# A hybrid mixer layer on one core: tokens added by accumulating transfers, DeltaNet's meta products and transposes over the whole array, scores in pieces of 24

## The chip, the cores and the metric

The kernel runs on one core of one Trainium2 chip. The metric is the device time of one execution in microseconds. Engines are named as in the profile: PE (TensorE matmul), PEld (TensorE weight load), DVE (VectorE), ACT (ScalarE), POOL (GpSimd), SP (SyncE, which here only issues transfers).

## The reference, cut to what matters

One layer with a residual add. 512 tokens of width 2048 are put behind 16 learned meta tokens, normalised, and projected to 7,585 columns that feed three mixers side by side: gated DeltaNet (6 heads), GLA (5 heads) and forgetting attention (5 heads). Their outputs, each times a SiLU gate, are concatenated to width 2048 and go through one output projection; its result is added to the tokens, and a final RMSNorm follows.

```python
h = rms_norm(x, norm_w)
proj = (h @ w_in).astype(f32)
...
o_dn  = gated_head_norm(gated_delta_rule_chunked(q_dn, k_dn, v_dn, log_a, beta), dz, dn_norm_w)
o_gla = gated_head_norm(gla_chunked(...), gz, gla_norm_w)
o_fox = forgetting_attention(...) * silu(fz)
o = concatenate([o_dn, o_gla, o_fox], -1)[:, PAD:]
return x + o @ w_out
```

The meta tokens are the first 16 of 528 columns in every mixer. For DeltaNet they give the state with which the first real block starts: `ym = (I + A)^-1 v`, then `state = k^T ym`, on 16 tokens. GLA's `attn` inside a block of 128 weighs each key dimension by a decay of its own; the kernel splits it by distance into levels of 64, 32, 16, 8, 4, 2, 1 and 0.

## The kernel before, in words

**Numbers.** All is float32. The large products run as three products of parts (high x high, low x high, high x low) in a type that TensorE streams at full rate. ScalarE makes the high part (`hp`, `ho`, `wh`: a cast), VectorE the low part (`lp`, `lo`, `wl`: a subtraction). Small products run in plain float32; the profile shows each of those as two matmul records.

**Order of the work.** (1) The tokens are loaded, scaled and split, and the first gate products run (`pz`, `pg`, `pbdz`, `pbgz`). (2) 18 pairs of 128-column projections run by Strassen's scheme with 7 instead of 8 products (`px`), about 94 to 477 us. For DeltaNet's q, k and v a convolution follows, and `token_rows` (line 725) turns each head's 128 x 528 result into rows of tokens: four transposes of 128 columns and, for k and v, one of the 16 meta columns, all into one bank of PSUM, with ScalarE copies between. (3) DeltaNet's triangular inverses are built by levels (`levels`, line 1110, `level64`, line 1154) and its four blocks are run (`state0`, line 1178, makes the state from the meta tokens; `core` and `tail` follow). (4) GLA and attention run, head by head; `gla_levels` (line 1377) emits the score products. In (3) and (4) sixteen single projections (`pbgq`, `pbfq`, `pbgz`, `pbfz`) fill TensorE between dependent steps. (5) The output projection has four column groups of 512. `OUT[0]` to `OUT[3]` take the first heads (`po`; three head pairs for groups 0 to 2, two for group 3), then one more head pair and Strassen products for the rest (`ps`) alternate, and a last product into the same banks as the running sum (`pz`) ends it. Each column group has four 128-token accumulators `acc[tb, cc]` in SBUF.

**Who sets the order.** A planner (`Weave`, line 237) writes out the program at build time. Each piece of work is a chain, a generator that yields operations, lists of operations, events or requests for buffers. The planner prices each operation (`cost`, line 206), tracks when its operands are ready, and picks the chain with the earliest start, where a chain's priority is added, and for TensorE a slack (0.25 us; 3.0 us for `token_rows`, line 854). What it emits is each engine's order on the chip; an engine that the plan misjudged waits there. Line 189 calls a TensorE operation light when it has fewer than 64 output columns or its weights have fewer than 128 rows or columns. Lines 343 to 356 gather light operations in runs: after 1.5 us of heavy work it takes a light operation whose planned ready time has come, and leaves light work when the run with the next list in it would be over 1.5 us long. A change to light costs 0.1 and back 0.2 us in the plan (line 268). A list that a chain yields is emitted as one piece.

**The places of the change.**

- `token_rows`: the meta transpose reads `c[:, 0:NM]`, 16 weight columns, and so is light.
- `dn_group` (line 1088) asks for tiles of `m_s` (16 slots of 128 x 384) and has SP load the meta tokens' values and keys into the first 16 rows of two of them.
- `state0`: three products of 16 x 16 by 16 x 128 (`pym<-vpm,um`), a ScalarE copy, three products with 16 rows (`pym<-ym,kdm`), a copy. All six are light.
- `gla_levels`: the score products are yielded in pieces of CH = 32 (line 92 sets it), two levels to a group; a group of the two small levels has 64 products for two heads, 32 for the last single head.
- `residual` (line 1882): for each accumulator SP loads the 128 x 512 tokens into `acc[tb, cc]`, and `e_res[cc]` tells that the four are there. `add_out` (line 1927) then adds the bank of `po` with VectorE and gives the bank back.
- `out_sums` (line 1801) has GpSimd issue accumulating transfers, 32 in all, that add weight matrices in HBM during stage (2).

Of the kernel before, what the change touches and what calls it, by code (L numbers as in the profile page):

```python
# [88 lines left out]
NXP, SQP, NSL = -0.6, 0.0, 1.5  # L89
LP, LSL = 0.1, 1.0  # L90
EXTRA = ()
NOP, CH, CD = 0, 32, 32
WP, AOP, HDP = 1.0, -0.6, 0.0
EARLY_KP = (3, 4)
STK, KOS, OS0, OSN, OSP = (3, 4, 6, 7), 3, 1, 2, 0.1
# [267 lines left out]
def tile_hybrid_trunk(ctx, tc, xT, xtok, mtok, w_gate, w_first, w_in, w_out, consts, lmask, fin_w, out):  # L363
# [361 lines left out]
    def token_rows(key, c, u):  # L725
        what, h = key
        g, j = divmod(h, H)
        blocks = [slice(b * P, (b + 1) * P) for b in range(NB)]
        dst, dstm, scale, acc_, ev = {"dk": (kds, kms, dl, nks, e_gate), "dv": (vps, vms, br, None, e_keys[g]),
                                      "dq": (None, None, None, nqs, e_gate)}[what]  # L730
        yield ev
        pk = yield Get(bank_s, f"pk{what}{h}", keep=2)
        yield [PE.transpose(pk[:, s], c[:, NM + s.start : NM + s.stop], ident) for s in blocks]
        if acc_ is not None:
            for b, s in enumerate(blocks):
                yield A.activation(u[:, s], pk[:, s], AF.Square, accum_out=acc_[:, b, h : h + 1])
        if dst is not None:
            for b, s in enumerate(blocks):
                yield A.activation(u[:, s], pk[:, s], AF.Copy, scale=scale[:, b, h : h + 1])
            yield SP.dma_start(out=dst[g].rearrange("p (b j) d -> p j b d", j=H)[:, j],  # L740
                               in_=u[:, :S].rearrange("p (b d) -> p b d", b=NB))
            yield PE.transpose(pk[:NM, :P], c[:, 0:NM], ident)
            m = c[:NM, P : 2 * P]
            if acc_ is not None:
                yield A.activation(m, pk[:NM, :P], AF.Square, accum_out=acc_[:NM, NB, h : h + 1])
            yield A.activation(m, pk[:NM, :P], AF.Copy, scale=scale[:NM, NB, h : h + 1])
            yield SP.dma_start(out=dstm[g][:, j], in_=m)
        bank_s.give(pk)
        row_s.give(c)
        sp_of(key).set()  # L750
        if what != "dv":
            {"dk": e_nk, "dq": e_nq}[what][h].set()
# [335 lines left out]
    def dn_group(g):  # L1088
        s = gs[g]
        if g:  # L1090
            yield e_first
        s.xc = yield Get(m_s, f"xc{g}", (P, NN, 32))
        yield e_inv
        yield SP.dma_start(out=s.xc, in_=sc2[N4 * g : N4 * g + N4].rearrange("(n r) (a c) -> (r a) n c", r=4, a=32))
        s.xm, s.um = one((32, H, 32), f"xm{g}"), one((32, H, 32), f"um{g}")
        yield SP.dma_start(out=s.xm, in_=sc2[M0 + H * g : M0 + H * g + H].rearrange("h (a c) -> a h c", a=32))
        s.kdm = yield Get(m_s, f"kdm{g}")
        s.vpm = yield Get(m_s, f"vpm{g}")
        for o, i in ((s.vpm[:NM], vms[g]), (s.kdm[:NM], kms[g])):
            yield SP.dma_start(out=o, in_=i)  # L1100
        yield e_anl[g]
        W.go(levels(g), -0.2, f"levels{g}", LSL)
        if not g:
            e_first.set()
# [5 lines left out]
    def levels(g):  # L1110
        s = gs[g]
        an, xc, xm, um = s.an, s.xc, s.xm, s.um
        uc = yield Get(m_s, f"uc{g}", (P, NN, 32))
        yield V.transpose(uc.rearrange("p n c -> p (n c)"), xc.rearrange("p n c -> p (n c)"))
        pm = yield Get(bank_s, f"pm{g}")
        p3 = pm[:, : NN * 32].rearrange("p (n c) -> p n c", c=32)
        lh = [(slice(64 * q, 64 * q + 32), slice(64 * q + 32, 64 * q + 64)) for q in range(2)]
        mm = [PE.matmul(p3[lo_, n, :], an[hi_, n, lo_], uc[hi_, n, :], start=True, stop=True)
              for n in range(NN) for lo_, hi_ in lh]
        for i in range(0, len(mm), CD):  # L1120
            yield mm[i : i + CD]
        m1 = yield Get(m_s, f"m1{g}", (P, NN, 32))
        for q in range(2):
            yield A.copy(m1[64 * q : 64 * q + 32], p3[64 * q : 64 * q + 32])
        W.go(state0(g), 0.0, f"state{g}")
        yield V.transpose(um.rearrange("p h c -> p (h c)"), xm.rearrange("p h c -> p (h c)"))
        e_um[g].set()
        mm = [PE.matmul(p3[a, n, :], l[lo_, n, :], r[lo_, n, :], start=True, stop=True)
              for n in range(NN) for lo_, hi_ in lh for a, l, r in ((lo_, xc, m1), (hi_, m1, xc))]
        for i in range(0, len(mm), CD):  # L1130
            yield mm[i : i + CD]
        l1 = yield Get(m_s, f"l1{g}", (P, NN, 32))
        yield A.copy(l1, p3)
        bank_s.give(pm)
        m_s.give(m1)
        s.uf = uf = yield Get(big_s, f"uf{g}", (P, NN, P))
        yield G.memset(uf, 0.0)
        for r in range(4):
            c = slice(32 * r, 32 * r + 32)
            yield A.copy(uf[c, :, c], uc[c])  # L1140
        m_s.give(uc)
        for q in range(2):
            yield V.tensor_copy(uf[64 * q : 64 * q + 32, :, 64 * q + 32 : 64 * q + 64], l1[64 * q : 64 * q + 32])
        eh = evs(0, 1)
        for q in range(2):
            W.go(level64(g, q, l1, eh[q]), -0.2, f"l64{g}{q}")
        yield (eh[0], eh[1])
        m_s.give(l1)
        m_s.give(xc)
        e_u[g].set()  # L1150
# [27 lines left out]
    def state0(g):  # L1178
        s = gs[g]
        yield (e_um[g], e_rows[g])  # L1180
        py = yield Get(bank_s, f"pym{g}")
        yield [PE.matmul(py[:NM, hc(j)], s.um[:NM, j, :NM], s.vpm[:NM, j, :], start=True, stop=True) for j in range(H)]
        ym = yield Get(m_s, f"ym{g}")
        yield A.copy(ym[:NM], h3(py)[:NM])
        m_s.give(s.vpm)
        yield [PE.matmul(py[:, hc(j)], s.kdm[:NM, j, :], ym[:NM, j, :], start=True, stop=True) for j in range(H)]
        st = yield Get(m_s, f"s0{g}")
        yield A.copy(st, h3(py))
        bank_s.give(py)
        m_s.give(ym)  # L1190
        m_s.give(s.kdm)
        s.so, s.f = one((P, NB, H), f"so{g}"), one((P, NB, H), f"f{g}")
        W.go(core(g, st), -0.3, f"core{g}")
# [538 lines left out]
    def phase_d():  # L1732
        yield e_c
        W.go(residual(), 0.0, "residual")
        for h in range(DN_HEADS):
            W.go(finish(h, gs[h // H].kd.rearrange("p (b j) d -> p j b d", j=H)[:, h % H], None), -0.05, f"split{h}")
        yield tuple(e_head[h] for h in range(DN_HEADS))
        e_split.set()
        for g in range(2):
            for q in range(3):  # L1740
                r_s.lend(gs[g].kd[:, 4 * q : 4 * q + 4, :].rearrange("p n d -> p (n d)"))
        for kp in ST:
            W.go(seven_heads(kp), HDP, f"heads{kp}")
        W.go(seven_loads(), -0.3, "sloads")
        W.go(seven_operands(), -0.45, "sops")
        yield tuple(e_z[i] for kp in ST for i in (2 * kp, 2 * kp + 1)) \
            + tuple(e_head[i] for kp in LATE for i in (2 * kp, 2 * kp + 1)) + (e_fin,)
        sweep()
        e_d.set()
# [50 lines left out]

    def out_sums():
        for i, (cp, kp) in enumerate((cp, kp) for cp in range(2) for kp in ST):
            p, q = pairs[OS0 + OSN * i : OS0 + OSN * i + 2]
            yield p.done[1]
            t = osum[cp, ST.index(kp)]
            (a, b), (c, d) = (tuple(w_out[2 * cp + n, kp][:, k * S : (k + 1) * S] for k in range(2)) for n in range(2))
            for n, w in ((5, c), (7, d), (6, d), (4, b)):
                yield SP.dma_start(out=t[:, SUMS.index(n)], in_=w)
            for n, w, ev in ((5, a, p.done[6]), (7, c, p.done[7]), (6, t[:, SUMS.index(5)], q.done[1]),
                             (4, t[:, SUMS.index(6)], q.done[6])):  # L1810
                yield ev
                yield G.dma_start(out=t[:, SUMS.index(n)], in_=w, accum_op=ALU.add)
# [69 lines left out]
    def residual():  # L1882
        for cc in range(4):
            for tb in range(4):
                yield OUT[cc][min(1 + tb // 2, len(OUT[cc]) - 1)].op
                acc[tb, cc] = yield Get(op_s, f"acc{cc}{tb}", (P, S), F32)
                yield SP.dma_start(out=acc[tb, cc], in_=xtok[tb * P : (tb + 1) * P, cc * 512 : (cc + 1) * 512])
            e_res[cc].set()

    e_res = evs(*range(4))  # L1890
# [8 lines left out]
    def mm_out(items):  # L1899
# [16 lines left out]
                    yield mm3(ps[tb], wj, oparts[2 * it.kp + j, tb], it is items[0] and j == 0, it is items[-1] and j == 1)  # L1916
            used(w)
        for tb in range(4):
            W.go(add_out(tb, cc, ps[tb]), AOP if cc != 2 else -0.6, f"add{tb}{cc}")
        if items is OUT[3]:  # L1920
            for h in range(DN_HEADS - 2):
                for t in dparts[h]:
                    op_s.give(t)
            yield tuple(e_res.values())
            op_s.move(d_s)

    def add_out(tb, cc, ps):
        yield from add(tb, cc, ps)
# [187 lines left out]
```

## Time and profile before

| | us |
|---|---|
| median of 3 runs | 963.39 (963.23 to 964.7) |
| the profiled execution | 963.21 |
| its span, first to last instruction | 961.4 |
| PE busy in the span | 948.3 |
| DVE busy | 738.5 |
| ACT busy | 581.2 |
| POOL busy | 66.1 |

Busy time of PE counts every stretch in which a matmul is in flight. Matmuls overlap, so the distance between the starts of two matmuls tells more than their durations: a short gap in the queue hides behind the end of the matmul before it. In the order of time each row is the start, the length, the engine, the instruction with what it writes and reads, and in brackets an idle time before it with what ended it. A shape such as 128*16 stands for the rows and columns of the weights. All rows carry line 285, the planner's emitter, so groups are told apart by their tiles.

### The profile page before, as it was taken

What the parts mean: (1) busy time and instruction counts of PE and PEld (TensorE: products, weight loads), DVE (VectorE), ACT (ScalarE), POOL (GpSimd) and SP (SyncE); (2) the same over time, 40 slices, a digit from 0 to 9 for tenths busy, and PEclk for the clock granted to TensorE, in tenths of its full rate; (3) what the DMA queues carried; (4) which work ended last, traced back from release to release, by engine and by line L of the source; (5) the groups of instructions that cost most, each with busy time, mean ns of one, the idle gap of its engine ahead of it and who ended that gap; (6) DMA issues with size and microseconds to landing.
All of it is one profiled execution on the core that took longest, in us unless ns stands there. A gap on an engine that the chain in (4) does not pass through costs nothing.

```text
span 961.4 us, 19098 instructions
## 1 busy us (share of the span) xinstructions
PE 948.3 (99%) x7283; PEld 844.6 (88%) x7283; DVE 738.5 (77%) x1308; ACT 581.2 (60%) x1243; POOL 66.1 (7%) x118
## 2 busy tenths in 40 slices
PE   9999999999999999999999999999999999999996
PEld 7888999999999999999987898878778878888885
DVE  7976888888888887888883665785765886887774
ACT  7855466757756575754432775848737756355445
POOL 0000101001101010110001110101010100000000
PEclk9999999999999999999999999999999999999998
DMA  9933647557786668783178545334323364565414
GB/s 348 367 121 132 162 136 219 163 183 197 198 239 151 208 150 224 183 241 93 67 255 297 167 95 172 135 101 146 117 95 111 130 213 154 195 230 174 151 59 176
DMA packets 92145, 167.20 MB, mean 174 GB/s; under 512 B 16253, under 2 KB 36477, under 8 KB 92052
## 3 DMA queue, kind: packets, MB, share of 16 engines
q1 hardware_dynamic: 87156, 157.31, 49.8%
q0 software_dynamic: 4608, 8.39, 6.3%
q8 instruction: 57, 0.93, 0.4%
q14 instruction: 36, 0.29, 0.1%
q10 hardware_dynamic: 288, 0.27, 0.1%
HBM read 142.33 MB, written 40.39 MB: 190 GB/s over the span
## 4 chain that ended last, share of the span: by engine, by line
PE 94%; DMA 2%; ACT 2%; DVE 1%; issue 0%; DVEq 0%; POOL 0%; SPq 0%; ACTq 0%; POOLq 0%
PE px L285 38%; PE po L285 10%; PE ps L285 8%; PE pbfz L285 6%; PE pz L285 6%; PE pbfq L285 5%; PE pbgz L285 5%; PE pbdz L285 2%; PE pks L285 2%; PE pfa L285 1%; PE pg L285 1%; PE pfw L285 1%; PE pss L285 1%; PE pbgq L285 1%; PE pgo L285 1%; DMA sc<-ab 1%
## 5 line engine op out<-in xcount | busy, mean ns | idle before, releaser
L285 DVE SCALAR_TENSOR_TENSOR lp<-a,hp 128x1024 fp32r<-128x1024 f32 x90 | 110.5, 1228 | 37.6 <-ACT hp L285 35.2
L285 ACT CAST hp<-a 128x1024 fp32r<-128x1024 f32 x90 | 94.5, 1049 | 72.4 <-PE px L285 45.4
L285 PE MATMUL px<-xh,hp 128*128 128x264 f32 x432 | 123.6, 286 | 0.0
L285 PE MATMUL px<-xh,lp 128*128 128x264 f32 x432 | 122.9, 285 | 0.0
L285 PE MATMUL px<-xl,hp 128*128 128x264 f32 x432 | 122.9, 285 | 0.0
L285 PE MATMUL px<-tah,hp 128*128 128x264 f32 x288 | 84.0, 292 | 0.0
L285 PE MATMUL px<-tbh,hp 128*128 128x264 f32 x288 | 82.5, 287 | 0.0
L285 PE MATMUL px<-tbh,lp 128*128 128x264 f32 x288 | 82.1, 285 | 0.0
L285 PE MATMUL px<-tah,lp 128*128 128x264 f32 x288 | 82.0, 285 | 0.0
L285 PE MATMUL px<-tbl,hp 128*128 128x264 f32 x288 | 81.9, 284 | 0.0
L285 PE MATMUL px<-tal,hp 128*128 128x264 f32 x288 | 81.8, 284 | 0.0
L285 PEld LDWEIGHTS px<-xh,hp 128*128 128x128 f32 x432 | 81.4, 188 | 0.0
L285 PEld LDWEIGHTS px<-xh,lp 128*128 128x128 f32 x432 | 81.3, 188 | 0.0
L285 PEld LDWEIGHTS px<-xl,hp 128*128 128x128 f32 x432 | 81.2, 188 | 0.0
L285 ACT CAST hp<-s 128x1024 fp32r<-128x1024 f32 x36 | 37.8, 1049 | 29.7 <-PE px L285 19.8
L285 PEld LDWEIGHTS px<-tbh,hp 128*128 128x128 f32 x288 | 54.3, 189 | 0.1
L285 PEld LDWEIGHTS px<-tbl,hp 128*128 128x128 f32 x288 | 54.3, 189 | 0.0
L285 PEld LDWEIGHTS px<-tah,hp 128*128 128x128 f32 x288 | 54.3, 188 | 0.1
L285 PEld LDWEIGHTS px<-tal,hp 128*128 128x128 f32 x288 | 54.3, 189 | 0.0
L285 PEld LDWEIGHTS px<-tah,lp 128*128 128x128 f32 x288 | 54.2, 188 | 0.0
L285 PEld LDWEIGHTS px<-tbh,lp 128*128 128x128 f32 x288 | 54.2, 188 | 0.0
L285 DVE SCALAR_TENSOR_TENSOR lp<-s,hp 128x1024 fp32r<-128x1024 f32 x36 | 44.0, 1222 | 8.4 <-ACT hp L285 8.4
(406 smaller groups left out, 2639.5 us busy)
## 6 DMA issues: line engine op xcount, KB each, us to landing
a<-in_w_in SPq DMA_DIRECT2D x72, 512.0 KB, 6.3
osum<-in_w_out SPq DMA_DIRECT2D x32, 256.0 KB, 6.2
o<-in_w_out SPq DMA_DIRECT2D x16, 512.0 KB, 3.6
kd<-osum SPq DMA_DIRECT2D x26, 256.0 KB, 3.6
kd<-in_w_out SPq DMA_DIRECT2D x21, 256.0 KB, 3.5
rgz<-in_w_in SPq DMA_DIRECT2D x10, 512.0 KB, 3.3
rfq<-in_w_in SPq DMA_DIRECT2D x10, 512.0 KB, 3.2
rfz<-in_w_in SPq DMA_DIRECT2D x10, 512.0 KB, 3.1
```

Of the source, the lines that this page charges most:

```text
L285: self.pin(op.call(*op.a, **op.kw))
```

## The change

The meta transpose takes the first 128 columns instead of 16 and writes 128 rows of the bank, of which 16 are read as before. The meta products of `state0` run on whole 128 x 128 operands: GpSimd zeroes three tiles, SP loads into two of them as before, and VectorE copies the 32 x 32 inverses into the third, `umf`. CH is 24 instead of 32. `residual` no longer loads the tokens; for the first products of each column group `first_out` has ScalarE copy the bank to `acc` and GpSimd issue a transfer that adds the tokens to it in SBUF. Two more constants are named or made fractional with the values as before.

```diff
-NOP, CH, CD = 0, 32, 32
+SPR = -0.45
+NOP, CH, CD = 0, 24, 32
...
-            yield PE.transpose(pk[:NM, :P], c[:, 0:NM], ident)
+            yield PE.transpose(pk[:, :P], c[:, 0:P], ident)
...
         s.vpm = yield Get(m_s, f"vpm{g}")
+        s.umf = yield Get(m_s, f"umf{g}")
+        for t in (s.umf, s.vpm, s.kdm):
+            yield G.memset(t, 0.0)
...
         yield V.transpose(um.rearrange("p h c -> p (h c)"), xm.rearrange("p h c -> p (h c)"))
+        yield V.tensor_copy(s.umf[:32, :, :32], um)
         e_um[g].set()
...
-        yield [PE.matmul(py[:NM, hc(j)], s.um[:NM, j, :NM], s.vpm[:NM, j, :], start=True, stop=True) for j in range(H)]
+        yield [PE.matmul(py[:, hc(j)], s.umf[:, j, :], s.vpm[:, j, :], start=True, stop=True) for j in range(H)]
         ym = yield Get(m_s, f"ym{g}")
-        yield A.copy(ym[:NM], h3(py)[:NM])
+        yield A.copy(ym, h3(py))
         m_s.give(s.vpm)
-        yield [PE.matmul(py[:, hc(j)], s.kdm[:NM, j, :], ym[:NM, j, :], start=True, stop=True) for j in range(H)]
+        m_s.give(s.umf)
+        yield [PE.matmul(py[:, hc(j)], s.kdm[:, j, :], ym[:, j, :], start=True, stop=True) for j in range(H)]
...
                 acc[tb, cc] = yield Get(op_s, f"acc{cc}{tb}", (P, S), F32)
-                yield SP.dma_start(out=acc[tb, cc], in_=xtok[tb * P : (tb + 1) * P, cc * 512 : (cc + 1) * 512])
             e_res[cc].set()
...
-            W.go(add_out(tb, cc, ps[tb]), AOP if cc != 2 else -0.6, f"add{tb}{cc}")
+            W.go((first_out if items in OUT else add_out)(tb, cc, ps[tb]), AOP if cc != 2 else -0.6, f"add{tb}{cc}")
...
+    def first_out(tb, cc, ps):
+        yield e_res[cc]
+        a = acc[tb, cc]
+        yield A.copy(a, ps)
+        bank_s.give(ps)
+        yield G.dma_start(out=a, in_=xtok[tb * P : (tb + 1) * P, cc * 512 : (cc + 1) * 512], accum_op=ALU.add)
+        need[tb, cc] -= 1
```

More of the change, by code (lines that the diff above doesn't have):

```diff
@@ L1744, in phase_d @@
         W.go(seven_loads(), -0.3, "sloads")
-        W.go(seven_operands(), -0.45, "sops")
+        W.go(seven_operands(), SPR, "sops")
         yield tuple(e_z[i] for kp in ST for i in (2 * kp, 2 * kp + 1)) \
@@ L1802, in out_sums @@
         for i, (cp, kp) in enumerate((cp, kp) for cp in range(2) for kp in ST):
-            p, q = pairs[OS0 + OSN * i : OS0 + OSN * i + 2]
+            p, q = pairs[OS0 + int(OSN * i) : OS0 + int(OSN * i) + 2]
             yield p.done[1]
```

## The prediction

> **What bounds the kernel now.** I read the page first, then the table of stages, then the chain of waits, then the order of time at the places the change touches.
>
> ```profile
> span 961.4 us, 19098 instructions
> ...
> PE 948.3 (99%) x7283; PEld 844.6 (88%) x7283; DVE 738.5 (77%) x1308; ACT 581.2 (60%) x1243; POOL 66.1 (7%) x118
> ```
>
> The profiled execution took 963.21 us, 1.8 us more than its span and 0.18 us less than the median of the three runs, 963.39 us. The sum below is made against 963.21 us. TensorE has work in flight in all but 13 us, most of that at the two ends. So the time can only change with what TensorE's own queue costs: matmul spacing, changes of array shape, and waits inside that queue.
>
> ```profile
> 590.00:771.00 181.00, 178.61 (x1723) 143.52 (x1722) 128.57 (x351) 121.32 (x325) 14.81 (x31) 1.00 0.39 129
> 808.00:852.00 44.00, 44.00 (x193) 35.65 (x192) 36.38 (x60) 18.59 (x28) 0.00 (x0) 1.00 0.51 167
> ```
>
> The columns of the table of stages are the stretch, its length, then the busy time of PE, PEld, DVE, ACT and POOL, the granted clock, the DMA share and GB/s. The GLA and attention stage (590 to 771) leaves TensorE idle for 2.39 us. The output stage (808 to 852), where the accumulating transfers will go, leaves it idle for nothing. GpSimd does nothing there.
>
> **The change part by part.**
>
> *Meta transposes (12, one per DeltaNet key and value head).* Two places in order of time (start, us, engine, work), the first without a wait, the second with one:
>
> ```profile
> 351.35 0.28 PE L285 MATMUL px<-xh,lp 128*128 128x264 f32 x1
> 351.47 0.27 PE L285 MATMUL pkdv<-ident,cv 128*16 128x128 f32 x1
> 351.50 0.36 PE L285 MATMUL px<-xh,hp 128*128 128x264 f32 x1
> 351.70 0.28 PE L285 MATMUL px<-xl,hp 128*128 128x264 f32 x1
> ```
>
> ```profile
> 316.88 0.28 PE L285 MATMUL px<-tah,lp 128*128 128x264 f32 x1
> 317.32 0.28 PE L285 MATMUL pkdv<-ident,cv 128*16 128x128 f32 x1 [0.15 <-ACT u L285]
> 317.35 0.37 PE L285 MATMUL px<-tah,hp 128*128 128x264 f32 x1
> 317.55 0.28 PE L285 MATMUL px<-tal,hp 128*128 128x264 f32 x1
> ```
>
> At 351 it is 0.35 us from the px before the transpose to the second px after it. One px takes 0.12 (351.47 less 351.35), so 0.35 is two px and 0.11 us for the transpose. A 16-column transpose inside a stream of whole-array matmuls therefore costs no more than its own streaming. At 317 the same stretch takes 0.67 us: 0.32 us more, and the bracket names ScalarE's evacuation u. So what these transposes cost is a wait, not their shape.
>
> The Trainium skill says otherwise: "TensorEngine Tiling (Array Packing)", Key Properties, has TensorE drain whenever the tiling mode changes. By that rule each of the 12 would win a pair of switches; the rows at 351 do not show one, and the measurement decides here.
>
> The wait comes from the planner, which writes out TensorE's order. A chain of transposes has a slack of 3.0 us (line 854), so that a chain is picked only when its operands have been ready for a while. But an operation with under 128 weight columns is "light" (line 189). After 1.5 us of heavy work, line 353 picks any light operation whose planned ready time has come, without the slack. And the plan is optimistic here: line 224 prices a 128-element ScalarE copy at 0.21 + 128 x 0.00082 = 0.315 us.
>
> ```profile
> L285 ACT ACTIVATE u<-pkdk,dl 128x128 f32<-128x128 f32 x24 | 7.2, 392 | 0.0
> ...
> L285 ACT ACTIVATE u<-pkdv,br 128x128 f32<-128x128 f32 x24 | 6.9, 368 | 0.6 <-PE pkdv L285 0.6
> ```
>
> ```profile
>   PEld pkdk L285: 0.2, 1
> ```
>
> ```profile
>   PEld pkdv L285: 1.1, 3
> ```
>
> Four such copies precede each meta transpose, so ScalarE ends 4 x 0.053 to 4 x 0.077 = 0.21 to 0.31 us after the plan's time, and TensorE, there on time, waits that long. The last two rows (from the views of the two tiles: who waited for ScalarE's copies, in total and how often) show four such waits of 1.3 us together. With 128 weight columns the transposes are heavy and get the 3.0 us of slack, like the block transposes beside them, which the copies cannot then be late for. Gain: between nothing (the waits land on other work) and 1.3 us; I take 1.2, since the copies are late by 0.3 us and the slack is ten times that. The added weight columns load while the matmul before streams. What the slack costs: a bank and a row buffer are held up to 3 us longer, with nobody in line for them as long as the next pair's convolution comes later than that; I count nothing, and what would be lost if it came sooner is part of the second rival.
>
> *Meta products of DeltaNet (24 matmul records in four groups of six).*
>
> ```profile
> 523.08 0.40 PE L285 MATMUL pbgz<-xh,lbgz 128*128 128x512 f32 x1
> 523.41 0.82 PE L285 MATMUL pym<-vpm,um 16*16 16x128 f32 x6
> 524.16 0.50 PE L285 MATMUL pbgz<-xh,hbgz 128*128 128x512 f32 x1
> 524.50 0.39 PE L285 MATMUL pbgz<-xl,hbgz 128*128 128x512 f32 x1
> ```
>
> ```profile
> 529.22 0.86 PE pym L285 x6
> ...
> 542.27 0.67 PE pks L285 x6
> ...
> 896.96 39.05 PE ps L285 x168
> ```
>
> The second fence is of the chain of waits (start, length, work). It prices whole-array work: 0.67 us for six products of 128 columns, 39.05/168 = 0.232 us for a matmul of 512. The first group stands alone between whole-array matmuls: 523.08 to 524.50 is 1.42 us, where two pbgz and six full products would take 2 x 0.232 + 0.67 = 1.13. Here the change of shape does cost: 0.29 us, in and out together. The others stand next to tiled work that stays, so only their own piece shrinks, from 0.86 to 0.67 in the one shown: 0.19 each at most. The sum lies between 0.29 and 0.29 + 3 x 0.19 = 0.86; I take 0.7 (1.2 if all four gain as the first does). The zeroing and the copy into the padded tile are new:
>
> ```profile
> L285 POOL MEMSET uf<- 128x1536 f32 x2 | 2.8, 1379 | 82.6 <-DMA sc<-ab 82.6
> ```
>
> Each new memset has a quarter of these elements, so between 0.34 and 1.38 us, three ahead of each group's loads, on an engine that had just waited 82.6 us for the inverse. SP's loads of the two meta tiles now wait for GpSimd, and behind them in SP's queue stands group 1's load of the inverse: 1.0 to 4.1 us late. The pbgz pieces around these products are filler that the planner puts into such gaps, so TensorE doesn't see it; without that cover it would cost those microseconds once. The same holds for the tile that now takes one more of 16 slots, and for the copy into it. Counted at nothing.
>
> *Scores in pieces of 24.* The planner prices a 32-wide product at 0.028 us and a run of light work at 1.5 us. Pieces of 32 (0.90 + 0.1 for the switch) do not fit twice, so 64 products run as 32 and 32. Pieces of 24 do (0.10 + 0.67 + 0.67 = 1.44), then 16 in a second run. The number of runs stays two a group, and one for the last pair of heads (24 + 8).
>
> ```profile
> 704.11 1.41 PE pbgz L285 x6
> 705.52 0.69 PE pss L285 x48
> 706.21 1.60 PE pbgz L285 x6
> ```
>
> Six pbgz behind a run take 1.60 instead of 1.41; with the entry as seen at 523 (0.33 from the last pbgz to the first small product instead of 0.23) a run costs 0.3 us beyond its products. The number of runs stays, so zero. Bounds: two runs fewer, -0.6; each of the nine groups split once more, +2.7, which the arithmetic of 1.44 under 1.5 excludes for all but accidents.
>
> *Tokens by accumulating transfers.* 16 vector adds leave, 16 ScalarE copies and 16 GpSimd transfers come, 16 SP loads go.
>
> ```profile
> L285 DVE TENSOR_TENSOR acc<-acc,po 128x512 f32<-128x512 f32 x28 | 17.8, 685 | 2.2 <-PE po L285 2.2
> ```
>
> ```profile
> L285 ACT COPY vt<-pvgv 128x512 f32<-128x512 f32 x5 | 2.9, 584 | 0.0
> ```
>
> ```profile
> osum<-in_w_out POOLq DMA_DIRECT2D x16, 256.0 KB, 6.4
> ```
>
> ```profile
> 845.36 2.48 DVE L285 TENSOR_TENSOR acc<-acc,po 128x512 f32<-128x512 f32 x4
> ```
>
> VectorE saves 16 x 0.685 = 11 us, ScalarE gains 16 x 0.584 = 9.3. Both have room (36.38 and 18.59 of 44 us), and TensorE has no gap there. A bank is free after 0.58 instead of 0.685 us. Accumulating transfers of this size land 6.4 us after their issue, here into HBM; into SBUF is not shown. The last four follow the last four adds, from 845.36. Even one strictly after another they land by 848 + 4 x 6.4 = 874 us, and the next add to those columns comes with the ps work that starts at 896.96. Counted at nothing (0.3 either way for the banks).
>
> Sum: 1.2 + 0.7 + 0 + 0 = 1.9 off the profiled execution's 963.21 is 961.3. A tenth, one bank's 0.1 us, for the case that TensorE reaches one of them too early makes it 961.2, which is 2.2 under the median. Own range: from 0 (no wait gone, first group only, banks against it) to 3.4 (1.3 + 1.2 + 0.6 + 0.3), 959.8 to 963.2.
>
> **The rivals.**
>
> *Waits elsewhere go too.* TensorE's order is planned anew from the first transpose on.
>
> ```profile
> L285 PE MATMUL pkd<-vt,kdt 128*128 128x128 f32 x30 | 4.4, 281 | 1.1 <-DVE gst L285 1.0 <-ACT gst L285 0.2
> ```
>
> Of the 2.39 us idle in 590 to 771 this one product has 1.1. A new order can lose about 2: 959.2. For: such waits exist only because plan and chip disagree. Against: nothing in the change aims at them.
>
> *They come back.* The same the other way, 2 us more: 963.2, no change. For: the slack moves every evacuation of the meta tokens, and with it bank and row buffer.
>
> *Every shape change drains.* If each of the 12 transposes saved the 0.29 us seen at the products, the sum would be 12 x 0.29 + 0.7 = 4.2: 959.0. The rows at 351 speak against it. It is the rule of the Trainium skill named above.
>
> *Slower: ScalarE at the ends of output columns.*
>
> ```profile
> L285 ACT CAST ho<-o 128x1024 fp32r<-128x1024 f32 x14 | 14.7, 1050 | 25.9 <-PE po L285 18.2 <-issue 5.9 <-PE pbfz L285 1.7
> ...
> L285 ACT CAST oh<-gz 128x512 fp32r<-128x512 f32 x5 | 2.7, 617 | 2.9 <-DVE gz L285 2.9
> ```
>
> ```profile
> L285 DVE SCALAR_TENSOR_TENSOR lo<-o,ho 128x1024 fp32r<-128x1024 f32 x14 | 17.1, 1224 | 10.0 <-ACT ho L285 8.6 <-DMA fw<-in_fin_w 1.2
> ```
>
> A weight operand lasts TensorE 24 x 0.232 = 5.57 us; the next needs a cast of 1.05 and a subtraction of 1.22. Four copies ahead make it 2.34 + 1.05 + 1.22 = 4.61, still in time. If five head casts (3.1) queue there too it is 7.7, a wait of 2.1 at each of four columns: 961.2 + 8.4 = 969.6. It decides once more than 0.96 us of other casts stand ahead. Against: ScalarE was busy 18.59 of 44 us there.
>
> **How the numbers follow.** A measurement of this kernel tells about 0.2%, 1.9 us: faster means under 961.46. Forecast 0.50, of which 0.30 falls under that line, as its centre stands 0.3 beneath it. Waits elsewhere go too 0.19, every shape drains 0.06 (both faster). They come back 0.18 (same). ScalarE late 0.07 (slower). That makes 0.55, 0.38 and 0.07. The range takes in the fast rivals' centres with 0.4 to spare and the scores' accidents on the slow side, and leaves out the slow rival and the rest of the fast tails: 958.6 to 963.7.
>
> **What would show it.** Right: the rows pkdk and pkdv with 128*128 alone and no PEld wait for u; pym at 128*128 with about 0.67 us a group; some 15 pss runs behind the first ones, each followed by six-matmul pieces of 1.60; po in one piece of 0.232 us a record; accumulating transfers landed well before acc's next add. Wrong: more pss runs than before, new waits for gst, y or pl, a gap in po, or transposes still waiting.

## The result and the profile after

| | before, us | after, us |
|---|---|---|
| median (11 runs each, taken on one chip) | 963.39 (962.49 to 964.99) | 966.87 (964.12 to 970.53) |
| the profiled execution | 963.21 | 965.08 |
| its span | 961.4 | 963.3 |
| its mean granted clock | 0.997 | 0.995 |

The ratio after to before is 1.0036, interval 1.0025 to 1.0048. The change makes the kernel slower; 961.2 was predicted, with 963.7 as the upper end. The page of after begins:

```profile
span 963.3 us, 19082 instructions
...
PE 945.8 (98%) x7283; PEld 844.5 (88%) x7283; DVE 728.8 (76%) x1294; ACT 588.5 (61%) x1259; POOL 85.7 (9%) x140
```

TensorE has 2.5 us less work in flight than before and yet ends later, so it stands still somewhere. The table of stages, with the two stages of the prediction and the stretch of DeltaNet's inverses:

```profile
520.00:548.00 28.00, 23.64 (x434) 19.39 (x433) 11.53 (x34) 16.73 (x35) 4.01 (x7) 0.94 0.55 161
590.00:771.00 181.00, 177.36 (x1697) 141.95 (x1696) 126.54 (x345) 118.98 (x319) 17.71 (x34) 1.00 0.41 134
808.00:852.00 44.00, 43.92 (x195) 35.45 (x194) 30.51 (x53) 29.59 (x58) 9.75 (x11) 1.00 0.76 203
```

The first of these rows for before:

```profile
520.00:548.00 28.00, 27.83 (x471) 21.96 (x470) 14.37 (x36) 19.24 (x38) 1.86 (x4) 1.00 0.62 205
```

From 520 to 548 TensorE had been idle for 0.17 us and is now idle for 4.36, and the granted clock, full before, is 0.94. GLA and attention lose 3.64 instead of 2.39 us; the output stage loses next to nothing (0.08), as predicted. The chain of waits names the place (start, length, what; the counts are those of the records on the chain, not of all). After:

```profile
521.47 3.83 DMA xc<-sc
...
525.39 0.59 DVE uc L286
...
526.02 0.95 PE pm L286 x48
526.97 1.58 PE pbfq L286 x6
528.55 0.95 PE pm L286 x66
529.50 1.53 PE pym L286 x12
531.04 0.52 PE pm L286 x41
531.56 3.17 issue
534.73 0.96 PE pm L286 x49
535.69 2.69 PE pbfq L286 x6
```

Before:

```profile
515.32 4.97 DMA xc<-sc
...
520.94 0.95 PE pm L285 x48
...
523.48 0.75 PE pym L285 x6
...
525.81 0.95 PE pm L285 x66
...
528.34 0.88 PE pm L285 x48
...
534.10 0.95 PE pm L285 x66
535.05 1.58 PE pbfq L285 x6
...
537.46 0.75 PE pym L285 x6
...
544.47 0.86 PE pym L285 x6
```

`pm` are the 32 x 32 products that build the inverses, per group a list of 48 records (`pm<-uc,an`) and one of 96. Before, the four lists lie from 520.9 to 535.1, with full products between every two. After, VectorE can turn the loaded inverses (`uc`) only later, group 0's by 3.9 and group 1's by 2.0 us. Before:

```profile
520.31 0.58 DVE L285 STREAM_TRANSPOSE uc<-xc 128x384 f32<-128x384 f32 x1 [3.74 <-DMA xc<-sc]
523.40 0.58 DVE L285 STREAM_TRANSPOSE uc<-xc 128x384 f32<-128x384 f32 x1 [1.04 <-DMA xc<-sc]
```

After:

```profile
524.22 0.58 DVE L286 STREAM_TRANSPOSE uc<-xc 128x384 f32<-128x384 f32 x1 [3.83 <-DMA xc<-sc]
525.39 0.58 DVE L286 STREAM_TRANSPOSE uc<-xc 128x384 f32<-128x384 f32 x1 [0.59 <-DMA xc<-sc]
```

The groups are now ready 1.2 instead of 3.1 us apart, and the lists stand close from 524.9 to 535.7: the two short ones together, six `pbfq`, and the two long ones with the `pym` between. In the last of them TensorE stops for 3.17 us, and the row says "issue": it waited for nothing that the profile shows. In TensorE's own view of waits it is the longest of all:

```profile
PE pm L286 <- issue: 3.2, 1, 3.2
PE pkd L286 <- DVE gst L286: 1.9, 2, 1.0
```

Behind the stop six `pbfq` take 2.69 instead of 1.58 us. In the order of time they start 0.43 us apart, where the same product otherwise takes 0.23:

```profile
536.21 0.63 PE L286 MATMUL pbfq<-xl,hbfq 128*128 128x512 f32 x1
536.64 0.63 PE L286 MATMUL pbfq<-xh,lbfq 128*128 128x512 f32 x1
```

That is about half the clock, and the granted clock agrees (it stands behind the busy times):

```profile
534.64:538.06 3.42, 3.33 (x58) 2.64 (x57) 1.32 (x4) 2.28 (x5) 0.35 (x1) 0.50 0.04 12
```

The stop with what follows it costs 3.17 + (2.69 - 1.58) + 0.3 (52 `pm` records start within 0.72 us behind it, 44 within 0.40 ahead of it) = 4.6 us. Without it the profiled execution would have taken 965.08 - 4.6 = 960.5, 0.7 under the prediction. The 1.87 us between the profiled executions are then 4.6 here and 1.25 in GLA and attention, less 4.0: 0.7 at the start and 0.8 behind the last matmul, where nothing was changed, and 2.5 in between.

**The theories.** TensorE's instructions come by a queue of their own:

```profile
q8 instruction: 57, 0.93, 0.4%
```

57 packets of 0.93 MB, 16 KB each, for 14,566 matmuls and weight loads: one packet for about 256 instructions. Counted from 0 over TensorE's rows in order, these and the waits for semaphores among them, the stop lies behind number 8128 = 256 x 30 + 448, and the trace has packet 30 on its way from 532.55 to 533.51. In ordinary stretches the transfer of packet n starts when TensorE is at about 256 n + 150 to 220. Theory 1: the packet was late, because 96 records of `pm` go by in under 1 us. Theory 2: the products themselves stop (operands, banks, load). Theory 3: the loss lies in the new order of the work behind 560 us. (Numbered as in the expectations of the later runs. In those of the first six, theory 2 is late data by the zeroing and the loads behind it, and theory 3 the copies and accumulating transfers at the end.)

### The profile page after: what moved, and what is told of

Read it like the earlier page. It is cut to its first block, busy times and chain, and to the rows that moved or that the text cites. A ratio compares the mean times of both kernels' runs of the same rounds, so it can differ in the third digit from the quotient of the medians.

```text
span 963.3 us, 19082 instructions
## 1 busy us (share of the span) xinstructions
PE 945.8 (98%) x7283; PEld 844.5 (88%) x7283; DVE 728.8 (76%) x1294; ACT 588.5 (61%) x1259; POOL 85.7 (9%) x140
## 4 chain that ended last, share of the span: by engine, by line
PE 92%; DVE 3%; ACT 2%; DMA 1%; issue 1%; SPq 0%; DVEq 0%; POOL 0%; ACTq 0%; POOLq 0%
PE px L286 38%; PE po L286 9%; PE ps L286 8%; PE pbfq L286 6%; PE pz L286 6%; PE pbgz L286 5%; PE pbfz L286 4%; PE pbdz L286 2%; PE pbgq L286 2%; PE pks L286 2%; PE pfa L286 1%; PE pg L286 1%; PE pfw L286 1%; PE pgo L286 1%; PE pss L286 1%; DMA sc<-ab 1%
```

## The experiments

Times are medians; the ratio is to the kernel before on the same chip.

**Each part alone, and all but the first.** Four kernels with one part of the diff each, and one without the transposes.

```diff
-            yield PE.transpose(pk[:NM, :P], c[:, 0:NM], ident)
+            yield PE.transpose(pk[:, :P], c[:, 0:P], ident)
```

> The kernel before with only the whole-array meta transposes. Theory 1, the supply of instructions: with these transposes no longer light, the planner puts the two groups' small pm products close together, and TensorE uses up the instructions that it has at hand; it stands still for 3 to 4 us inside a list of pm products with nothing that it waits for, and its clock is halved for a few us after it. Less the 1.2 us of the waits for u: 965.5 to 967 us. Theory 2, late data at DeltaNet's start (zeroing on GpSimd, loads behind it): nothing of that is here, 962.2 us. Theory 3, ScalarE copies and accumulating transfers at the end: 962.2 us.

> The kernel before with only the padded meta products of state0 and their zeroing. Theory 1: the pm lists stay as far apart as before, no stall, 962.7 us (0.7 less). Theory 2: the stall of 3 to 4 us in pm comes with the zeroing and the later loads, 966 us. Theory 3: 962.7 us.

> The kernel before with only the score pieces of 24. Theories 1 and 2: as many runs of pss as before, 963.4 us, within 1 us. A rival for the 1.5 us that the GLA stage lost: the pieces move the waits for gst and fp, 965 us.

> The kernel before with only the tokens added by accumulating transfers. Theories 1 and 2: TensorE's queue is the same up to the output stage, 963.4 us, within 0.5. Theory 3: 3 us more, 966.4 us, with gaps between po matmuls behind 796 us.

> The changed kernel with the meta transposes left at 16 columns. Theory 1 (supply of instructions): the pm lists are 7 us of other work apart again, no stall; 962 to 963 us. Theory 2 (late data at DeltaNet's start by zeroing and loads): the stall stays, 966 us.

| | us | ratio | interval |
|---|---|---|---|
| transposes alone | 975.5 | 1.0127 | 1.0112 to 1.0142 |
| meta products alone | 962.0 | 0.9989 | 0.9979 to 0.9999 |
| pieces of 24 alone | 976.55 | 1.014 | 1.0127 to 1.0153 |
| tokens alone | 962.64 | 0.9996 | 0.9988 to 1.0005 |
| all but the transposes | 974.28 | 1.0121 | 1.0106 to 1.0136 |

The parts don't add up: two of them cost 12 and 13 us alone, and all four together 3.5. These two and the kernel with all but the transposes lie 8 to 12 us over what was expected. TensorE's waits with the transposes alone:

```profile
PE pm L285 <- issue: 2.3, 1, 2.3
PE ps L285 <- ACT wh L285: 1.7, 1, 1.7
```

With pieces of 24 alone:

```profile
PE pfa L285 <- ACT fp L285: 7.8, 4, 6.4
```

The stop in `pm` goes with the transposes: it is in the changed kernel and in this one, both at number 8128, and in none of the other four (at the border of packet 29 the meta products alone have 0.4 us, all but the transposes 0.3). The transposes alone bring neither zeroing nor copies nor accumulating transfers, so theories 2 and 3 of the first six expectations can't be what makes it. The other losses are waits for ScalarE and VectorE at places that the change doesn't touch. Pieces of 24 move the last attention head's softmax in among the output products, where VectorE has sums of weights and of outputs ahead of it in its queue; TensorE waits 6.4 us up to 810.3. The kernel with all but the transposes has the same wait (6.7 us), the changed kernel doesn't. Part of the losses is the clock: it is half for 13.7 us with the transposes alone and for 10.2 with pieces of 24, against 3.4 in the changed kernel and none in the one before (all ahead of 950 us). So a new order cost up to 13 us, whatever the edit was for, and the same transposes that cost 12 alone gained 7 on top of the other three parts.

**The lists kept apart.** The changed kernel, with group 1's first list held back in the plan until group 0's second has been evacuated.

```diff
+        if g:
+            yield e_l1
         pm = yield Get(bank_s, f"pm{g}")
...
+        if not g:
+            e_l1.set()
```

> The changed kernel, but group 1's first pm list waits in the plan for group 0's second one. No computation is left out, no data comes sooner. Theory 1: no stall, and the clock stays up: the changed kernel's time less 3.4 us of stall and 1 to 1.5 of slow clock, 960 to 962 us. Theory 2: group 1's data are as late as before and TensorE waits for them as long, 965 to 967 us.

Measured: 961.58 (960.74 to 963.44), 0.9985 (0.9977 to 0.9994), the lowest median of all (the meta products alone, 0.9989, are level with it), 5.3 under the changed one (4.9 by the ratios). Its chain has no stop in `pm`:

```profile
528.72 0.95 PE pm L285 x66
...
531.23 0.88 PE pm L285 x48
532.10 2.31 PE pbfq L285 x9
...
535.95 0.68 PE pm L285 x50
```

This speaks for theory 1, but it can't exclude 3, since the order behind is planned anew too.

**Twice the products, in one list or in pieces.** In the kernel before, group 1's second list is issued twice, as one list of 192 records or in pieces of 64. (In the kernel with one list, group 0's second list goes out whole as well.)

```diff
+        again = [PE.matmul(p3[a, n, :], l[lo_, n, :], r[lo_, n, :], start=True, stop=True)
+              for n in range(NN) for lo_, hi_ in lh for a, l, r in ((lo_, xc, m1), (hi_, m1, xc))]
+        mm = again + mm if g == 1 else mm
```

> The kernel before; group 1's 48 second-level pm products are issued twice into the same places (the same values), and all 96 stand in one list. Theory 1: 384 weight loads and matmuls of 7 to 9 ns each in a row are more than TensorE has at hand; it stands still for 2 to 4 us in the midst of the list, at a multiple of 256 instructions, 967 to 969 us. A supply that is not the limit: only the added 96 records at 9 ns, 964.3 us.

> The kernel before with the same 48 added products, but in pieces of 32, between which the planner puts other matmuls. Theory 1: as many instructions, but spread over 5 us and more, so no stall or one under 0.5 us: 0.9 us for the products and 0.3 to 0.6 for the changes of shape, 964.6 to 965 us. If the added work and not its density counted: the same time as the kernel with the 96 in one list.

Measured: 975.5 (1.0139, 1.0122 to 1.0157) and 971.55 (1.0085, 1.0072 to 1.0099). TensorE's longest wait with the one list:

```profile
PE pm L285 <- issue: 2.8, 1, 2.8
```

The stop comes in the one list, at number 8384 = 256 x 31 + 448, and not in pieces, as expected. Both times are 6 us and more over what was expected. Most of both losses is again in waits elsewhere, so the times say little; a test that leaves the order alone was needed.

**The numbers shifted, the order kept.** In these kernels every engine's order is the same as in the kernel they are made from; only TensorE's warm-up at the start is altered: four of its nine full products give way to small ones, unknown to the plan. Each small one is 4 instructions, so the borders of the packets move against the work.

```diff
-        yield [PE.matmul(pw[:, :P], ones, ones, start=True, stop=True) for _ in range(9)]
+        mm = [PE.matmul(pw[:, :P], ones, ones, start=True, stop=True) for _ in range(5)]
+        for o in mm:
+            o.dur *= 9 / 5
+        yield mm
+        q = slice(0, 32)
+        for _ in range(24):
+            W.pin(nc.tensor.matmul(pw[q, q], ones[q, q], ones[q, q], start=True, stop=True))
```

> The changed kernel with the same order of all work; only the warm-up ahead of the first product differs: 5 full products in place of 9, then 24 products of 32*32, so that every later instruction of TensorE has a number higher by 80 (weight loads and matmuls counted alike). The place where a packet of 256 instructions must have come then lies 80 instructions earlier in the work: 4.8 us of work instead of 3.2 lie between the call for packet 30 and its use. Theory 1 (the standstill inside pm is a late packet of instructions): the standstill goes or falls under 1 us, and with it the halved clock behind it; about 962.5 us (961 to 964), 0.995 to 1.000 of the changed kernel's 966.9 or less, hence level with the kernel before. Theory 2 (the standstill belongs to the products themselves, their operands, banks or load): it stays at the same product, 3 us long, and the time stays at 966.9. Theory 3 (the order behind 560 us costs it): 966.9 as well, with the waits of the GLA stage as they were.

> The same with 44 small products, so that the numbers rise by 160. Packet 30 is then needed before the dense part, but packet 31 in it: 3.1 us of work lie between its call and its use. Theory 1: the standstill is back, 2.5 to 3.5 us long, at instruction 256*31+448 = 8384 of TensorE's rows, which is another product than in the changed kernel (224-160 = 96 instructions later in the work); time 965 to 968. Theory 2: it stays at the same product as in the changed kernel. Theory 3: 966.9 in all cases, and no tie to the numbers.

> The kernel before with the whole-array transposes of the meta tokens alone (975.5 us), with the warm-up changed as above so that the numbers rise by 80; the order of all other work stays. 5.5 us of work then lie between the call for packet 30 and its use instead of 3.9. Theory 1: the 2.5 us standstill in pm goes with its slow clock, 3 to 4 us, to about 972; the rest of its loss, the waits for ScalarE and VectorE at 645 to 750 and at 861 to 864, stays, since the order stays. Theory 2: 975.5 with the standstill in place.

Measured: 965.19 (1.0023, 1.0013 to 1.0032), 972.86 (1.0095, 1.0083 to 1.0107) and 972.72 (1.0101, 1.0085 to 1.0117). With 80 the stop is gone, but not by the shift alone: the clock is half from 529.98 to 533.39, between the short and the long lists, and stretches the work in question from the expected 4.8 to 6.2 us. With 160 it is back at number 8384, as expected, at another product than in the changed kernel:

```profile
PE pm L286 <- issue: 2.3, 1, 2.3
```

The two times missed. The altered warm-up costs too much, as the start with 80 shows, and with 160 the clock is also half for 10.2 us from 530.95 on:

```profile
3.56 2.77 PE L537 MATMUL warm<-ones 32*32 32x32 f32 x48
6.26 2.08 PE L286 MATMUL pz<-xh,fhi 128*128 128x512 f32 x4
8.13 1.91 PE L286 MATMUL pz<-xl,fhi 128*128 128x512 f32 x4
```

The first real product starts at 6.26 instead of 5.16 us, and eight of them need 0.45 us each where the full clock gives 0.23. The transposes alone came out near what was expected: 2.8 us less (2.5 by the ratios) with the stop gone, and the waits at 861 us unchanged; here too the clock was half, from 529.58 to 532.99, ahead of the long lists.

**Five and nine products more.** The full warm-up stays, and small products come behind it.

```diff
         yield [PE.matmul(pw[:, :P], ones, ones, start=True, stop=True) for _ in range(9)]
+        q = slice(0, 32)
+        for _ in range(5):
+            W.pin(nc.tensor.matmul(pw[q, q], ones[q, q], ones[q, q], start=True, stop=True))
```

> The changed kernel with nothing taken out and five products of 32*32 added behind the nine full products of the warm-up (10 records, 20 instructions of TensorE); the order of all other work stays. The warm-up with 24 small products had cost 1.1 us at the start and some 2 more because the slow clock lasted longer, which hid what the standstill gave back; five behind the full warm-up cost 5 x 0.116 = 0.6 us and should not hold the clock back. Packet 30 is now needed 20 instructions earlier in the work, with 4.5 us of work behind its call instead of 3.2. Theory 1 (late packet): the kernel with the added products is faster than the changed kernel: no standstill over 1 us in pm, about 963 us (962 to 964.5), level with the kernel before. Theory 2 (the products or the order): 966.9 + 0.6 = 967.5, standstill in place.

> The changed kernel with nine small products behind the full warm-up (36 instructions of TensorE); the order of all other work stays. 4.6 us of work behind the call for packet 30, as with 20 instructions (4.5), and a border 16 instructions further from the dense part. Theory 1 (late packet): at most as many long executions as with five products (3 of 12), median 962.9 (0.4 for four products more), and in the profile, if its time is under 964, no standstill over 0.7 us in pm. Theory 2 (chance, or the warm-up itself): a standstill in the profile although the time is low, or a median near 966.9.

> The kernel before with the same five products behind the warm-up. If these only move the borders of the packets: 0.6 us more than before, 963.6 (963.2 to 964.2), since no packet is late in it with or without them (5.4 us of work behind the scarcest call). If the five products by themselves speed up the start or the clock, as a rival to theory 1: about 959, 4 us less than before.

> The changed kernel with scores in pieces of 32 again; the other parts stay. Theory 1: the lists of pm stand in one stretch as in the changed kernel (2.9 us of planned work behind the call for packet 30), so the standstill is there, 2.5 to 3.4 us at instruction 8128, and the time is 965 to 968. Rival: the pieces of 24 cost 3 us or more on their own in this company too, and without them the time falls to about 963 with the standstill in place.

| | us | ratio | interval |
|---|---|---|---|
| after, five more | 962.5 (961.23 to 966.72) | 1.0001 | 0.9991 to 1.0011 |
| after, nine more | 963.52 (961.93 to 965.33) | 1.0 | 0.9991 to 1.0009 |
| before, five more | 964.34 (963.61 to 966.08) | 1.0005 | 0.9996 to 1.0014 |
| after, pieces of 32 | 970.23 (969.12 to 971.06) | 1.0063 | 1.005 to 1.0075 |

Five products that do no work make the changed kernel 4.4 us faster (3.4 by the ratios), with the same order of everything else. In the kernel before the same five gain nothing (0.7 more, and 0.6 was expected), so the altered warm-up isn't what helps. As the cause of the 3.5 us theories 2 and 3 fall here: products, operands and order are those of the changed kernel. Two points missed. With five products the stop was expected to fall to 1 us or less, with nine to 0.7, and the profile with nine more (the median execution) still has half of it. For nine products, a stop in the profile of a fast execution had been put down as the sign of a rival, that the low time is chance or the warm-up's own, and that sign came:

```profile
532.65 1.61 issue
...
535.06 1.58 PE pbfq L286 x6
```

What is gone is the slow clock behind it: six `pbfq` in 1.58 us. The profiled execution with five more (966.7) is one of four long ones among twelve (964.6 to 966.7; the other eight took 961.2 to 962.8), and has the slow clock:

```profile
532.80 1.70 issue
...
535.22 2.11 PE pbfq L286 x6
```

With pieces of 32 the stop stands at 8128 as expected (2.8 us in the view of waits), but the time is 2 over the expected range, with other waits and a second stretch of half the clock (527.25 to 530.66); the pieces of 24, 13 us dear alone, save 3.4 in this company (2.6 by the ratios).

What decides between a late packet and chance is the place. In the traces of all 17 kernels, every wait of a TensorE product over 0.4 us that the profile puts down to "issue" stands there: eleven stops of 0.43 to 3.17 us, in `pm`, `pym`, `pss` and `po`, each right behind a number that is a multiple of 256 plus 448 or 449. How much of the gain with five and nine products is the shorter stop (1.5 us) and how much the clock, which fell behind one of the two stops and not behind the other, rests on single executions.

One table over the traces puts the packets together. "Call" is where TensorE reaches number 256 n + 140, a number chosen a little ahead of where the transfers start in ordinary stretches; "next" is the product behind number 256 n + 448.

| kernel, packet | stop | work behind the call, us | call to next | packet landed to next |
|---|---|---|---|---|
| after, 30 | yes | 3.2 | 6.56 | 1.22 |
| after, pieces of 32, 30 | yes | 3.5 | 6.51 | 1.24 |
| transposes alone, 30 | yes | 3.9 | 6.38 | 1.44 |
| after, five more, 30 | yes | 4.6 | 6.45 | 1.27 |
| after, nine more, 30 | yes | 4.6 | 6.44 | 1.31 |
| after, counted on by 160, 31 | yes | 2.9 | 5.33 | 1.40 |
| before, doubled in one list, 31 | yes | 1.3 | 4.26 | 1.30 |
| before, doubled in pieces, 31 | no | 4.6 | 4.64 | 1.66 |
| after, counted on by 80, 30 | no | 6.2 | 6.18 | 2.70 |
| lists apart, 30 | no | 6.9 | 6.94 | 2.25 |
| before, 30 | no | 8.0 | 8.04 | 3.17 |

In the seven kernels that stop, the next product starts 1.2 to 1.4 us behind the landing, however much work there was; in the four without a stop it starts later than that. The stop is what the work lacks of the time from the call to there. That time is no constant: 6.4 to 6.6 us for packet 30, 5.3 and 4.3 for packet 31 in two other kernels, and 4.6 us of work were enough in one and too little in two. Why the transfer of a packet sometimes starts later is not known.

## Why the prediction was wrong

**The step that failed** is the first: "So the time can only change with what TensorE's own queue costs: matmul spacing, changes of array shape, and waits inside that queue." There is a fourth cost, the supply of instructions, and the prediction put it at nothing. It moved lists of tiny products without asking how many instructions TensorE would then use up in a few microseconds. It cost 3.17 us in the profile, and with the slow clock behind it 4.6. Spacing the lists gave 5.3 back, and five idle products 4.4 (4.9 and 3.4 by the ratios).

**Meta transposes, -1.2.** Mechanism right. TensorE's wait for ScalarE's copies at `pkdv` fell from 1.1 us in three to this, and that at `pkdk` is gone:

```profile
  PEld pkdv L286: 0.3, 1
```

That is 1.0 of 1.3 us. The stretch of the `px`, in which all these transposes and otherwise the same products stand, got as much shorter. Before, then after (first and last start):

```profile
L285 PE MATMUL px<-xh,hp x432: 279/284/374, 94.5 to 473.9; 128*128 128x264 f32 x144
L286 PE MATMUL px<-xh,hp x432: 279/284/390, 93.8 to 472.2; 128*128 128x264 f32 x144
```

From the first `px` of any kind to the last it is 397.3 and 396.2 us, 1.1 less. Over all 17 kernels of this case it is 397.2 to 398.9 us with the narrow transposes and 395.7 to 397.0 with the wide ones. What the slack holds up, "I count nothing", may not have been free: with the transposes the inverses come 3.9 and 2.0 us later and the lists close up. That the banks are the reason isn't shown.

**Meta products, -0.7.** Mis-sized in this company. The four `pym` pieces of the chain took 0.75 + 0.86 + 0.75 + 0.86 = 3.22 us before and take 2 x 1.53 = 3.06 (the second pair lies at 543.04, as long). They now stand between tiled lists, so the changes of shape that they were to remove stay, and the pieces gain 0.16 us. Alone they measured 0.9989, 1.1 us, with an interval that ends just short of no change.

**Their cover.** "The planner puts filler into such gaps, so TensorE doesn't see it" wasn't even put to the test by the zeroing: GpSimd is done with that by 492.5, 26 us ahead of the loads, so these don't wait for it. Ahead of the lists TensorE does wait for `uc`, 1.2 us in two waits, and with the transposes alone, where nothing is zeroed, 1.6.

**Scores, 0.** TensorE enters the score products 18 times before and after, as worked out. But a new order is not free of cost: +13 alone, -3.4 in company (-2.6 by the ratios).

**Tokens, 0.** Right: 0.9996, and the two new rows are as priced, 0.584 and 6.4 us predicted, 0.589 and 6.8 measured.

```profile
L286 ACT COPY acc<-po 128x512 f32<-128x512 f32 x16 | 8.9, 589 | 2.5 <-PE po L286 1.7
...
acc<-in_xtok POOLq DMA_DIRECT2D x16, 256.0 KB, 6.8
```

**The rivals.** "They come back" came nearest: a new order brought the loss, but by a stop for instructions and not by the waits for data that it named, and not in its size: 2 us were given to it, and parts alone showed 12 and 13. "ScalarE at the ends of output columns" didn't come. "Every shape change drains" didn't either: 12 x 0.29 = 3.5 us would have gone from the stretch of the `px`, and 1.1 went. With the stop taken away by spacing, the sum is near the forecast, 961.58 measured and 961.2 predicted. That is in part luck: the terms within it differ, and GLA and attention, planned anew, still lose 3.12 us instead of 2.39.

Why the transposes let the inverses come later is not settled; the plan is made anew from the first transpose on. Which of the waits behind 560 us a given order brings was read from the traces, not tested.

## What to carry to other kernels

Count the instructions, not only the microseconds: a stop that waits for nothing, always at the same distance behind a multiple of 256 instructions, was a late packet here, and long products between the lists of tiny ones cured it. Where a planner writes the order, price each edit by the spread of its reorderings (here 13 us) beside its own sum, and test a suspected cause with edits that leave the order alone. A part that is dear alone can be cheap in company and the other way round, so measure the whole, and then mend its one worst wait.

## What the runs showed of the hardware

Instructions arrive while the kernel runs, in 57 packets of 16 KB for TensorE. The Trainium skill ("Trainium Architecture — The Big Picture", The software stack) has the streams moved into each engine's instruction memory when the program is loaded; the packet on its way from 532.55 to 533.51 shows that this isn't all, and the measurement decides.

A stop of 3.17 us among tiny products was followed by half the clock until 538.06 in the changed kernel, one of 1.70 us with five products more by half the clock from 536.06 to 542.89, and one of 1.61 us with nine more by none. The Trainium skill ("TensorE: Matmul & The Clock Gate", HAM oscillation) puts the limit at idle gaps of about 3.4 us. These runs don't bear it out as the only one: 3.17 is a little under it, 1.70 well under, and with the numbers raised by 80 the clock is half from 529.98 on behind 96 records of `pm` and a wait of 1.2 us, without any stop. That the tiny products count as little activity would explain it, and also the late full clock behind a warm-up with 48 records of them; no run tests it alone. The slow stretches between 500 and 950 us last 3.4, 6.8 or 10.2 us, one, two or three times the same length.

The changed kernel's executions spread over 6.4 us, those with the lists apart over 2.7. Mean granted clocks were 0.988 to 0.996 in the one and 0.996 to 0.998 in the other, and the longest execution, 970.53, has the lowest clock: the spread goes largely with the clock.
